# A modulation stream stepped more slowly, and attention's first scores put ahead of the last value transposition

## The chip, the cores and the metric

The kernel runs on one core of a Trainium2 chip. A core has a matrix engine (PE), a vector engine (DVE), a scalar engine (ACT), GpSimd (POOL) and a sync engine (SP) that here issues nearly all DMAs. Each engine takes its instructions strictly in the order in which they were written; engines wait for one another by semaphores. The metric is device time in microseconds (us). Before the change the median of three runs was 2344.88 us (2339.64 to 2345.45).

## The reference, cut to what matters

The program is a transformer block followed by two more mixing layers. Only the first block's first half matters here. With x of 1024 positions by 1024 channels:

```
mod = silu(c) @ w_ada + b_ada                 # 6 x 1024 numbers: shifts, scales, gates
h = modulate(rms_norm(x), mod[0], mod[1])
proj = h @ w_in                               # 25 blocks of 128 columns
o_a = gated linear attention of 4 heads       # q, k, v, r and decay blocks of proj
o_b = softmax attention of 4 heads            # Q, K, V blocks; two score maps a head, a bias on each
x = x + mod[2] * (concat(o_a, o_b) @ w_out)
...                                           # feed-forward with mod[3..5], then the second block
```

The first two parts of `mod` are needed at once. The other four (32 blocks of 128 numbers) are first needed after the softmax attention.

## The kernel before, in words

**phase1** (L428) computes the 25 blocks of `h @ w_in`. Each is 48 fp32r matmuls of 512 columns (L214) into one of two PSUM tiles `ps_g`, and an evacuation (`evac1`, L629) on ACT and DVE: a high part (`ehi`) and a low part (`elo`), which go to DRAM. A `V` block is first copied to an SBUF tile `vt` by ACT, later transposed on PE (`ps_v`, L660) and then split. The last two blocks are K and V of head 3: for these the first half of the columns is done for both, then the second half.

Two background streams are interleaved with these matmuls. Every second contraction step calls `tick`, which lowers each stream's waiting count by its rate; when it is used up, the stream takes one step, and the step says how long to wait for the next one. Stream `bg` runs the heads of the linear attention (`gla_head`): decays by a scan on DVE, exponentials on ACT, small matmuls, a state recurrence of 30 DVE instructions (`sx`), and the output `uh`, `ul`. Stream `bg2`, with rate 0.6, runs the modulation (`ada`, L364): 32 steps, each of which issues the load of the *next* 512 KB weight tile `adw` on SP (two buffers) and then takes one dot product on DVE from the tile that was loaded a step ago (called a dot below). A step returns 2.0, so dots are at least 2.0/0.6 ticks apart.

Between the two halves of the last two blocks, SP issues eight loads for the softmax attention's head 0 (`load_head`) and two biases (`load_bias`). At the end, the last value block's transposition is done (`pend.pop()()`, L607), then `drain` (L608) runs whatever the two streams still have, without matmuls between, and the pools of phase 1 are closed.

**phase2** (L827) is the softmax attention, in 32 steps of 128 queries. `scores` issues 8 matmuls into the two `ps_g` tiles (there called `ps_s`); `expo` adds the bias on DVE (`s`, with the running extreme `mx`) and takes exponentials on ACT; `combine` works on POOL, then PE transposes and the products with the values follow.

Of the kernel before, what the change touches and what calls it, by code (L numbers as in the profile page):

```python
# [10 lines left out]
F32 = mybir.dt.float32  # L11
# [9 lines left out]
T = 1024  # L21
# [99 lines left out]
class Builder:  # L121
# [239 lines left out]
        src = self.bias_d[h, bass.ds(fl * (qb + 1), 1), :, bass.ds((1 - fl) * (128 * qb), T)]  # L361
        self.S.dma_start(out=out, in_=src.rearrange("a p c -> (a p) c"))

    def ada(self, src, n0, n, bias, pairs, pool):  # L364


        ws = deque()

        def load(i):
            if i < n:  # L370
                w = pool.tile([128, D], F32, tag="adw", name="adw", bufs=2)
                self.S.dma_start(out=w, in_=src[n0 + i])
                ws.append(w)

        load(0)
        yield 6.0
        for i in range(n):
            load(i + 1)
            w = ws.popleft()
            for j, (vec, out) in enumerate(pairs):  # L380
                o = w if j == len(pairs) - 1 else pool.tile([128, D], F32, tag="adt", name="adt", bufs=1)
                self.dot(o, w, vec, out[:, i:i + 1])
                yield 2.0 if o is w else 1.0
        for _, out in pairs:
            self.V.tensor_tensor(out=out, in0=out, in1=bias, op=ALU.add)
        yield
# [41 lines left out]
    def phase1(self):  # L428
        nc, tc, V, A, G, S, PE, I = self.nc, self.tc, self.V, self.A, self.G, self.S, self.PE, self.I
# [40 lines left out]
        for half, ps in enumerate(sums):  # L470
            for k in range(8):
                q = nmp.tile([128, 512], F32, tag="nm", name="sq")
# [72 lines left out]
        evp = gl.enter_context(tc.tile_pool(name="evp", bufs=4, reuse_waits="tile"))  # L545
# [14 lines left out]
        self.bg.rate, self.bg2.rate = 0.8, 0.6  # L560
        self.bg2.append(self.lam())
        crow = self.cond_row(self.cond_d, glp, "crow")
        self.bg2.append(self.ada(I["w_ada"], 16, 32, self.vec("b_ada", 16, 32), [(crow, self.mod[:, 16:48])], evp))
        pend = []

        def products(n, ps, **kw):
# [5 lines left out]
        def evac(n, ps):  # L572
            later = self.evac1(order[n], ps, evp)
            if later is not None:
                pend.append(later)

        for n in range(23):
            if n < 3:
                ps = ps0[n]
            else:  # L580
                ps = self.psg.tile([128, T], F32, tag="g", name="ps_g")
# [7 lines left out]
        for half in range(2):  # L589
            for j in range(2):  # L590
                products(23 + j, last[j], halves=(half,))
                if half:
                    self.release(23 + j)
                    evac(23 + j, last[j])
            if not half:
                self.hst[0].close()
                self.heads = {}
                self.hdst = ExitStack()
                self.hpools = [self.hdst.enter_context(tc.tile_pool(name="hdp0", bufs=1, side="right", reuse_waits="tile"))]
                for part in range(8):  # L600
                    self.load_head(0, part)

                self.fl = S.value_load(self.flag[0:1, 0:1], min_val=0, max_val=1)
                self.bias = {}
                for g in range(2):
                    self.load_bias(g, self.ring.tile(("bias", g), [128, T], F32, "bias"))
        pend.pop()()  # L607
        self.drain()  # L608
        gl.close()
        self.hst[1].close()  # L610
        ph.close()
# [17 lines left out]
    def evac1(self, what, ps, evp):  # L629

        nc, V, A, G, S, PE = self.nc, self.V, self.A, self.G, self.S, self.PE
        kind, i = what[0], what[1:]
        if what == "lr":
            self.lr = self.glp.tile([48, T], F32, name="lr")
            A.activation(out=self.lr, in_=ps[0:48], func=ACTF.Copy)
        elif kind in "qk":
            t = evp.tile([128, T], F32, tag="ev", name="ev")
            if kind == "q":
                A.activation(out=t, in_=ps, func=ACTF.Copy, scale=0.125)
            else:  # L640
                V.tensor_copy(out=t, in_=ps)
            S.dma_start(out=self.gqk_d["qk".index(kind), int(i)], in_=t)
        elif kind == "r":
            t = evp.tile([128, T], F32, tag="ev", name="ev")
            A.preload_act_table_set(SET_SILU)
            A.activation(out=t, in_=ps, func=ACTF.Silu)
            A.preload_act_table_set(SET_EXP)
            S.dma_start(out=self.gr_d[int(i)], in_=t)
        elif kind in "vV":


            vt = evp.tile([128, T], F32, tag="ev", name="vt")
            A.activation(out=vt if kind == "v" else vt[:, ::-1], in_=ps, func=ACTF.Copy)

            def later():
                pts = []
                for g in range(2):
                    pt = self.pst.tile([128, 4, 128], F32, tag="t", name="ps_v")
                    for b in range(4):
                        PE.transpose(pt[:, b], vt[:, (4 * g + b) * 128:(4 * g + b + 1) * 128], self.eye)  # L660
                    pts.append(pt)
                if kind == "v":
                    vn = evp.tile([128, 8, 128], F32, tag="ev", name="ev")
                else:
                    hi = evp.tile([128, T], F32R, tag="ev", name="ehi")
                    lo = evp.tile([128, T], F32R, tag="ev", name="elo")
                for g, pt in enumerate(pts):
                    if kind == "v":
                        A.activation(out=vn[:, 4 * g:4 * g + 4], in_=pt, func=ACTF.Copy)
                    else:  # L670
                        h3, l3 = (x[:, g * 512:g * 512 + 512].rearrange("p (b d) -> p b d", b=4) for x in (hi, lo))
                        A.activation(out=h3, in_=pt, func=ACTF.Copy)
                        V.tensor_tensor(out=l3, in0=pt, in1=h3.bitcast(F32), op=ALU.subtract)
                if kind == "v":
                    S.dma_start(out=self.gv_d[int(i)].rearrange("p (b d) -> p b d", b=8), in_=vn)
                else:
                    S.dma_start(out=self.v_d[int(i), 0], in_=hi.bitcast(F32))
                    S.dma_start(out=self.v_d[int(i), 1], in_=lo.bitcast(F32))
            return later
        else:  # L680
            self.split_out(ps, 0.125 if kind == "Q" else 1.0, self.qk_d[int(i), "QK".index(kind)], evp, kind == "K")
        return None
# [26 lines left out]
    def gla_head(self, hd):  # L709
# [114 lines left out]
        S.dma_start(out=self.oa_d[hd, 1], in_=ul.bitcast(F32))  # L824
        yield

    def phase2(self):  # L827

        nc, tc, V, A, G, S, PE = self.nc, self.tc, self.V, self.A, self.G, self.S, self.PE
# [4 lines left out]
        pool = lambda name, bufs, **k: at.enter_context(tc.tile_pool(name=name, bufs=bufs, reuse_waits="tile", **k))  # L834
# [1 line left out]
        bp, self.hvpool, sp, ap, cp = pool("bip", 2), pool("hdv1", 1), pool("sp", 3), pool("atp", 2), pool("acp", 4)  # L836
        trp = at.enter_context(tc.tile_pool(name="trp", bufs=2, space=PSUM))
        NS = 32
        heads, bias, sc, aT, rc = self.heads, self.bias, {}, {}, {}

        def scores(g):
            h, qb = divmod(g, 8)
            q, *kk = heads[h][:3]
            pss = []
            for m in range(2):
                ps = self.psg.tile([128, T], F32, tag="g", name="ps_s")
                for a in range(2):
                    for j in range(2):
                        PE.matmul(ps[:, a * 512:a * 512 + 512], lhsT=q[:, m, qb * 128:qb * 128 + 128],
                                  rhs=kk[j][:, m, a * 512:a * 512 + 512], start=j == 0, stop=j == 1)  # L850
                pss.append(ps)
            sc[g] = pss

        def expo(g):
            mx, sm = (cp.tile([128, 2], F32, tag=t, name=t) for t in ("mx", "sm"))
# [96 lines left out]
        for g in range(-3, NS + 2):  # L952
            if 1 < g + 3 < NS:
                self.load_bias(g + 3, bp.tile([128, T], F32, tag="b", name="bias"))
            if (g + 3) // 8 < 3:
                self.load_head((g + 3) // 8 + 1, (g + 3) % 8)
            if g in (2, 10, 18):
                self.n_max = len(self.seq)
                self.pump(g // 8, -1)
            if g >= 6 and g % 4 > 1 and part < 16:  # L960
                wo_part(part // 8, part % 8)
                part += 1
            if 0 <= g < NS:
                transp(g)
            if 0 <= g + 1 < NS:
                combine(g + 1)
            if 0 <= g - 2 < NS:
                values((g - 2) // 2, g % 2)
            for n in (0,):
                at_step(g, n)  # L970
            if g + 3 < NS:
                scores(g + 3)
            if 0 <= g + 2 < NS:
                expo(g + 2)
                bias.pop(g + 2)
                if g + 2 < 2:
                    self.ring.free(("bias", g + 2))
            if 0 <= g < NS:
                lows(g)
            for n in (4, 3, 2, 1):  # L980
                at_step(g, n)
# [1287 lines left out]
```

## Time and profile before

| | before |
|---|---|
| median of 3 runs | 2344.88 us |
| the profiled execution's own time | 2343.11 us |
| its span | 2341.3 us |
| PE busy | 2188.7 us (93%) |
| DVE busy | 1489.8 us (64%) |
| POOL busy | 1000.9 us (43%) |
| ACT busy | 837.8 us (36%) |
| mean granted PE clock | 0.971 |

The span is what the profile covers; the execution's own time is 1.8 us longer. PE's share is an average over stages. A stage is therefore read by the time in which PE stands still in it, and by what released it. Times in the rows below are counted from the span's start; phase 1's matmuls end near 424 us and the softmax attention starts there.

### The profile page before, as it was taken

Reading aid. Unit: us, or ns where it says so; the run is one execution under the profiler, and the core shown is the slowest. Engines: PE = TensorE matmul, PEld = TensorE weight load, DVE = VectorE, ACT = ScalarE, POOL = GpSimd, SP = SyncE. Lnnn points to the kernel's source line nnn. Section 1 sums busy time; section 2 is a strip of 40 time slices with the busy share of each in tenths; the row PEclk is TensorE's granted clock in tenths of the full one; section 3 lists DMA queues with packets and bytes.
Section 4 is the critical chain, followed back from the end, with each engine's and each line's share of the span. In section 5 each row is a group of like instructions: output and inputs, shape, how many; then the busy total and the mean of one; then the engine's idle time right before and its main releaser. Section 6 shows DMA issues by size and latency. Waiting matters only on the chain. (4 is left out here: it accounts for less than half of the span.)

```text
span 2341.3 us, 28680 instructions
## 1 busy us (share of the span) xinstructions
PE 2188.7 (93%) x10168; PEld 1781.9 (76%) x10168; DVE 1489.8 (64%) x2480; ACT 837.8 (36%) x1371; POOL 1000.9 (43%) x790
## 2 busy tenths in 40 slices
PE   6999998799999999989999998797978999999998
PEld 3777776687877888878787876686866777788886
DVE  8674666589365866799867756849895746221124
ACT  4334332588443222122223335532322444222223
POOL 7333332499443332313465525545543553322243
PEclk8999999899999999999999999898989999999999
DMA  7265664984522344413232424463534624111143
GB/s 269 97 189 201 208 208 158 270 235 149 212 90 99 121 158 153 150 32 101 80 128 90 129 71 134 124 191 134 185 135 138 228 86 149 50 45 51 49 153 117
DMA packets 188838, 326.19 MB, mean 139 GB/s; under 512 B 46818, under 2 KB 87682, under 8 KB 188436
## 3 DMA queue, kind: packets, MB, share of 16 engines
q1 hardware_dynamic: 188400, 324.14, 42.3%
q8 instruction: 80, 1.31, 0.2%
q14 instruction: 66, 0.54, 0.1%
q10 hardware_dynamic: 292, 0.20, 0.0%
HBM read 260.71 MB, written 67.46 MB: 140 GB/s over the span
## 5 line engine op out<-in xcount | busy, mean ns | idle before, releaser
L59 POOL TENSOR_TENSOR lo<-raw,hi 128x512 fp32r<-128x512 f32 (+3 forms) x458 | 561.3, 1238 | 935.4 <-ACT hi L59 511.5
L59 ACT ACTIVATE hi<-raw 128x512 fp32r<-128x512 f32 (+3 forms) x462 | 244.9, 557 | 537.6 <-PE ps_o L214 165.9
L214 PE MATMUL ps_g<-h0hi,hi 128*128 128x512 f32 x568 | 228.5, 402 | 13.3 <-ACT h0hi L59 8.6
L214 PE MATMUL ps_g<-h0lo,hi 128*128 128x512 f32 x568 | 223.5, 393 | 4.7 <-POOL h0lo L59 4.7
L214 PE MATMUL ps_g<-h1lo,hi 128*128 128x512 f32 x568 | 223.4, 393 | 4.7 <-DVE h1lo L59 4.7
L214 PE MATMUL ps_g<-h1hi,hi 128*128 128x512 f32 x568 | 226.8, 399 | 0.0
L214 PE MATMUL ps_g<-h0hi,lo 128*128 128x512 f32 x568 | 223.3, 393 | 1.9 <-DVE lo L59 1.4
L214 PE MATMUL ps_g<-h1hi,lo 128*128 128x512 f32 x568 | 223.2, 393 | 0.0
L59 DVE SCALAR_TENSOR_TENSOR u<-ps_g,vecs,u 128x1023 f32<-128x1023 f32 (+3 forms) x94 | 114.1, 1214 | 93.1 <-ACT u L59 90.4
L214 PEld LDWEIGHTS ps_g<-h0hi,hi 128*128 128x128 f32 x568 | 108.2, 190 | 40.0 <-ACT h0hi L59 9.9
L214 PEld LDWEIGHTS ps_g<-h0lo,hi 128*128 128x128 f32 x568 | 107.8, 190 | 28.7 <-POOL h0lo L59 6.4
L214 PEld LDWEIGHTS ps_g<-h1lo,hi 128*128 128x128 f32 x568 | 107.8, 190 | 28.3 <-DVE h1lo L59 6.0
L214 PEld LDWEIGHTS ps_g<-h0hi,lo 128*128 128x128 f32 x568 | 107.8, 190 | 25.7 <-DVE lo L59 1.8
L214 PEld LDWEIGHTS ps_g<-h1hi,hi 128*128 128x128 f32 x568 | 107.6, 189 | 25.2 <-issue 2.5
L214 PEld LDWEIGHTS ps_g<-h1hi,lo 128*128 128x128 f32 x568 | 107.7, 190 | 22.9
L214 PE MATMUL ps_d<-acthi,hi 128*128 128x512 f32 x272 | 109.2, 401 | 12.0 <-DVE u L59 9.3
L59 DVE TENSOR_TENSOR acc<-acc,sq 128x512 f32<-128x512 f32 x69 | 76.1, 1105 | 52.6 <-ACT sq L59 51.0
L214 PE MATMUL ps_d<-actlo,hi 128*128 128x512 f32 x272 | 107.7, 396 | 0.0
L214 PE MATMUL ps_d<-acthi,lo 128*128 128x512 f32 x272 | 107.6, 396 | 0.0
L59 DVE TENSOR_TENSOR t<-ps_i,rot 64x480 f32<-64x480 f32 (+3 forms) x108 | 64.8, 600 | 38.9 <-PE ps_i L1487 32.7
L59 POOL TENSOR_TENSOR s<-s,s 128x1024 f32<-128x1024 f32 x32 | 77.1, 2410 | 2.7
L59 DVE CUSTOM_DVE_ANT_0 s<-ps_s,bias 128x1024 f32<-128x1024 f32 x64 | 75.7, 1217 | 2.8 <-DMA bias<-bias_d 2.2
(403 smaller groups left out, 5350.5 us busy)
## 6 DMA issues: line engine op xcount, KB each, us to landing
adw<-in_ada_w_dram SPq DMA_DIRECT2D x48, 512.0 KB, 3.5
raw<-in_w_up_dram SPq DMA_DIRECT2D x88, 256.0 KB, 2.8
adw<-in_w_ada_dram SPq DMA_DIRECT2D x32, 512.0 KB, 6.1
bias<-bias_d SPq DMA_DIRECT2D x32, 512.0 KB, 4.3
raw<-in_w_in_dram SPq DMA_DIRECT2D x50, 256.0 KB, 3.9
raw<-in_odd_w_in_dram SPq DMA_DIRECT2D x48, 256.0 KB, 2.6
raw<-in_even_w_in_dram SPq DMA_DIRECT2D x44, 256.0 KB, 4.0
raw<-in_w_down_dram SPq DMA_DIRECT2D x72, 128.0 KB, 2.5
```

Source lines behind the costliest of these rows:

```text
L59: return f(*a, **k)
L214: self.PE.matmul(out, lhsT=a[:, k], rhs=b, start=first and n == 0, stop=last and n == 2)
```

## The change

Three edits. (1) `ada` gets a parameter `lead`, and the first block's modulation stream passes 3.0 where the step's wait was 2.0; the second block's use keeps 2.0. (2) The last value block (`V3`) is copied by ACT into the linear attention's tile `w2` of the pool `glp`, not into one of the four rotating tiles `ev`. (3) `drain` runs first, then the scores of softmax step 0 are issued (the function became a method), and only then the last value block is transposed.

```diff
-    def ada(self, src, n0, n, bias, pairs, pool):
+    def ada(self, src, n0, n, bias, pairs, pool, lead=2.0):
...
-                yield 2.0 if o is w else 1.0
+                yield lead if o is w else 1.0
...
-        self.bg2.append(self.ada(I["w_ada"], 16, 32, self.vec("b_ada", 16, 32), [(crow, self.mod[:, 16:48])], evp))
+        self.bg2.append(self.ada(I["w_ada"], 16, 32, self.vec("b_ada", 16, 32), [(crow, self.mod[:, 16:48])], evp, lead=3.0))
...
+        self.drain()
+
+        self.sc = {}
+        self.scores(0)
         pend.pop()()
-        self.drain()
         gl.close()
...
-            vt = evp.tile([128, T], F32, tag="ev", name="vt")
+
+            end = what == "V3"
+            vt = self.glp.tile([128, T], F32, tag="w2", name="vt") if end else evp.tile([128, T], F32, tag="ev", name="vt")
...
+    def scores(self, g):
+
+        h, qb = divmod(g, 8)
+        q, *kk = self.heads[h][:3]
+        self.sc[g] = []
+        for m in range(2):
+            ps = self.psg.tile([128, T], F32, tag="g", name="ps_s")
+            for a in range(2):
+                for j in range(2):
+                    self.PE.matmul(ps[:, a * 512:a * 512 + 512], lhsT=q[:, m, qb * 128:qb * 128 + 128],
+                                   rhs=kk[j][:, m, a * 512:a * 512 + 512], start=j == 0, stop=j == 1)
+            self.sc[g].append(ps)
...
-            if g + 3 < NS:
-                scores(g + 3)
+            if 0 < g + 3 < NS:
+                self.scores(g + 3)
```

What this moves on the engines is shown at three places.

DVE, where head 3 of the linear attention begins, before: `w` from `ps_z` is the head's decay input, the `adw` rows are dots, the two `smask` rows are the scan, `elo` is the low part of a projected block.

```order
L59 TENSOR_SCALAR w_14932<-ps_z,vecs 128x1024
L59 ISA adw,mod<-adw,crow 128x1024
L59 ISA mod 128x1
L59 ISA adw,mod<-adw,crow 128x1024
L59 ISA mod 128x1
L59 SCALAR_TENSOR_TENSOR w_14974<-smask,w_14932 64x1024 x2
L59 COPY bl<-w_14974 64x16 x2
L59 SCALAR_TENSOR_TENSOR elo<-ps_g,ehi 128x1024
```

The same place on DVE after the change:

```order
L59 TENSOR_SCALAR w_14908<-ps_z,vecs 128x1024
L59 ISA adw,mod<-adw,crow 128x1024
L59 ISA mod 128x1
L59 SCALAR_TENSOR_TENSOR w_14947<-smask,w_14908 64x1024 x2
L59 COPY bl<-w_14947 64x16 x2
L59 ISA adw,mod<-adw,crow 128x1024
L59 ISA mod 128x1
L59 SCALAR_TENSOR_TENSOR elo<-ps_g,ehi 128x1024
```

The second dot has moved from ahead of the scan to behind it, still ahead of `elo`.

DVE at the end of phase 1, before: `mod<-mod` closes the modulation, `ul` ends the linear attention, and the last two rows are the low part of the last value block and the first bias addition of the softmax attention.

```order
L59 TENSOR_TENSOR mod<-mod,vecs 128x32
L59 SCALAR_TENSOR_TENSOR sx<-sx,dec,U 64x128 x6
L59 SCALAR_TENSOR_TENSOR elo<-ps_g,ehi 128x1024
L59 SCALAR_TENSOR_TENSOR w_15414<-ps_o,vecs,ki 128x1024
L59 TENSOR_TENSOR w_15414<-w_15414,sr 128x1024
L59 TENSOR_TENSOR ul<-w_15414,uh 128x1024
L59 TENSOR_TENSOR elo<-ps_v,ehi 128x512 x2
L59 ISA s_15520,mx<-ps_s,bias 128x1024
```

The same place after the change; where lines are left out stand seven more pairs of a dot and its `mod` row.

```order
L59 SCALAR_TENSOR_TENSOR elo<-ps_g,ehi 128x1024
L59 SCALAR_TENSOR_TENSOR w_15388<-ps_o,vecs,ki 128x1024
L59 TENSOR_TENSOR w_15388<-w_15388,sr 128x1024
L59 ISA adw,mod<-adw,crow 128x1024
L59 ISA mod 128x1
L59 TENSOR_TENSOR ul<-w_15388,uh 128x1024
L59 ISA adw,mod<-adw,crow 128x1024
L59 ISA mod 128x1
...
L59 TENSOR_TENSOR mod<-mod,vecs 128x32
L59 TENSOR_TENSOR elo<-ps_v,ehi 128x512 x2
L59 ISA s_15520,mx<-ps_s,bias 128x1024
```

Nine of the 32 dots now stand behind the linear attention's last products, eight of them behind `ul`, and all of them ahead of the first bias addition.

SP's queue at the same end, before, from the second bias on: `qk_d` are the parts of the last K block, `oa_d` the linear attention's output, `v_d` the last value block, `q` and `k` the softmax attention's head 1.

```order
L362 DMA bias<-bias_d 128x1024
L690 DMA qk_d<-ehi 128x1024
L691 DMA qk_d<-elo 128x1024
L823 DMA oa_d<-uh 128x1024
L824 DMA oa_d<-ul 128x1024
L677 DMA v_d<-ehi 128x1024
L678 DMA v_d<-elo 128x1024
L624 DMA q<-qk_d 64x2x1024
```

The same place after the change:

```order
L362 DMA bias<-bias_d 128x1024
L372 DMA adw<-in_w_ada_dram 128x1024
L695 DMA qk_d<-ehi 128x1024
L696 DMA qk_d<-elo 128x1024
L372 DMA adw<-in_w_ada_dram 128x1024
L828 DMA oa_d<-uh 128x1024
L829 DMA oa_d<-ul 128x1024
L372 DMA adw<-in_w_ada_dram 128x1024 x7
L682 DMA v_d<-ehi 128x1024
L683 DMA v_d<-elo 128x1024
L627 DMA q<-qk_d 64x2x1024
```

Nine weight loads stand behind the ten loads for the softmax attention, seven of them behind `oa_d<-ul`. On PE the only move is that the eight transposing matmuls of the last value block stand behind the eight of the first scores.

## Rows read from the trace of the kernel before

**Rows 1.** Busy time of each engine in two stretches of phases 1 and 2.
```profile
core 0: us, PE busy (x) PEld busy (x) DVE busy (x) ACT busy (x) POOL busy (x), PEclk, DMA share, GB/s
190.00:400.00 210.00, 197.38 (x999) 158.84 (x998) 132.09 (x191) 75.14 (x102) 72.53 (x40) 0.98 0.61 211
460.00:600.00 140.00, 136.42 (x850) 115.04 (x849) 117.86 (x235) 115.65 (x219) 123.32 (x100) 0.99 0.69 206
```
**Rows 2.** PE's instructions in order of time, 160 to 375 us: start, length, idle before.
```profile
217.70 0.82 PE L762 MATMUL ps_f<-qi,ki 64*128 64x128 f32 x5 [1.05 <-DVE ki L59]
...
251.67 0.66 PE L805 MATMUL ps_o<-qi,sx 128*128 128x64 f32 x4 [2.18 <-DVE sx L59]
...
365.04 0.50 PE L214 MATMUL ps_g<-h0hi,hi 128*128 128x512 f32 x1 [3.33 <-DVE elo L59]
...
371.35 1.43 PE L762 MATMUL ps_f<-qi,ki 64*128 64x128 f32 x5 [4.64 <-DVE ki L59]
```
**Rows 3.** All engines in order of time, 345 to 369 us (head 3's beginning).
```profile
347.24 2.43 POOL L59 TENSOR_TENSOR w<-w,w 128x1024 f32<-128x1024 f32 x1 [5.22 <-ACT w L59]
...
348.02 1.23 SPq L372 DMA_DIRECT2D adw<-in_w_ada_dram  x2
...
357.58 1.22 DVE L59 CUSTOM_DVE_ANT_0 adw<-adw,crow 128x1024 f32<-128x1024 f32 x1 [10.15 <-DMA adw<-in_w_ada_dram]
...
358.73 4.60 DVE L59 TENSOR_TENSOR_SCAN w<-smask,w 64x1024 f32<-64x1024 f32 x2
...
363.76 1.22 DVE L59 SCALAR_TENSOR_TENSOR elo<-ps_g,ehi 128x1024 fp32r<-128x1024 f32 x1
...
367.93 3.36 DVE L59 TENSOR_TENSOR ki<-k,ki 128x1024 f32<-128x1024 f32 x1
```
**Rows 4.** SP's DMA queue in order of time, 398 to 430 us.
```profile
403.99 0.65 SPq L624 DMA_DIRECT2D q<-qk_d  x1
...
409.92 2.47 SPq L362 DMA_DIRECT2D bias<-bias_d  x2
419.94 0.33 SPq L690 DMA_DIRECT2D qk_d<-ehi  x1
```
**Rows 5.** DMA issues, 400 to 445 us: count, KB each, us from issue to landing.
```profile
qk_d<-ehi SPq DMA_DIRECT2D x1, 512.0 KB, 9.5
```
**Rows 6.** The modulation's weight tile, 150 to 432 us: its DMAs.
```profile
DMA to landing us min/median/max: 3.4/6.1/10.1
```
**Rows 7.** All engines in order of time, 418 to 446 us (phase 1's end).
```profile
422.40 1.22 DVE L59 TENSOR_TENSOR w<-w,sr 128x1024 f32<-128x1024 f32 x1
...
429.53 1.02 ACT L59 ACTIVATE vt<-ps_g 128x1024 f32<-128x1024 f32 x1 [4.82 <-DMA qk_d<-ehi]
...
430.61 1.97 PE L660 MATMUL ps_v<-eye,vt 128*128 128x128 f32 x8 [6.54 <-ACT vt L59]
...
432.67 1.29 DVE L59 TENSOR_TENSOR elo<-ps_v,ehi 128x512 fp32r<-128x512 f32 x2 [6.70 <-PE ps_v L660]
...
434.32 1.23 DVE L59 CUSTOM_DVE_ANT_0 s<-ps_s,bias 128x1024 f32<-128x1024 f32 x1 [0.36 <-PE ps_s L849]
...
444.96 1.23 DVE L59 CUSTOM_DVE_ANT_0 s<-ps_s,bias 128x1024 f32<-128x1024 f32 x1 [2.23 <-DMA bias<-bias_d]
```
**Rows 8.** The second block's modulation, dots and loads in order of time, near 915 us.
```profile
914.18 1.22 DVE L59 CUSTOM_DVE_ANT_0 adw<-adw,cond 128x1024 f32<-128x1024 f32 x1
...
915.44 2.68 SPq L372 DMA_DIRECT2D adw<-in_ada_w_dram  x2
...
919.02 1.23 DVE L59 CUSTOM_DVE_ANT_0 adw<-adw,cond 128x1024 f32<-128x1024 f32 x1 [1.26 <-DMA adw<-in_ada_w_dram]
```
**Rows 9.** Busy time and granted clock in three short stretches, columns as in rows 1.
```profile
428.00:432.00 4.00, 1.39 (x7) 1.39 (x8) 0.00 (x0) 1.26 (x2) 0.00 (x0) 0.54 0.89 363
432.00:436.00 4.00, 4.00 (x13) 3.01 (x12) 2.81 (x5) 1.29 (x3) 0.00 (x0) 0.60 0.50 202
436.00:440.00 4.00, 2.12 (x9) 1.12 (x8) 2.65 (x7) 2.30 (x5) 1.12 (x1) 1.00 1.01 246
```

More of the change, by code (lines that the diff above doesn't have):

```diff
@@ L838, in phase2 @@
         NS = 32
[L839 to L852, printed above, removed]
+        heads, bias, sc, aT, rc = self.heads, self.bias, self.sc, {}, {}
         def expo(g):
```

## The prediction, made before the changed kernel was timed

> **What bounds the kernel now.** I read the busy time by stretches first, then PE's own order of time for the places where it stood still, then what DVE, SP's queue and the DMAs did at those places. PE is busy 197.38 of 210 us in the middle of phase 1 and 136.42 of 140 us in the softmax attention [rows 1]: in both stages it is PE that sets the pace. So an edit gains only what it takes out of PE's idle time, and a start of the softmax attention that is late by some amount is not made good later, since PE has 3.6 us of slack in 140.
>
> In phase 1 the idle of PE that DVE causes lies at a few places [rows 2]: 1.05 us for `ki`, 2.18 us for the recurrence `sx`, then 3.33 us for an `elo` and 4.64 us for `ki` of head 3. The two last have one cause. A dot had its load issued at 348.02 and started only at 357.58, after 10.15 us in which DVE did nothing; scan, `elo`, `qi` and `ki` stand behind it [rows 3]. At the end, PE waits 6.54 us for the copy `vt`, and that for a rotating tile, until the write `qk_d<-ehi` has landed (4.82 us) [rows 7].
>
> **Change part by part.** *The slower stream, in phase 1.* The number of dots is the same, 32; nine of them move out of phase 1's matmuls to its end. What that frees, place by place:
>
> - Head 3's beginning. The scan needs POOL's `w`, done at 347.24 + 2.43 = 349.67. Without a second dot ahead of it, scan and its small copies take 349.7 to 354.7 (in the old place 358.73 to 363.76, 5.03 us) [rows 3]. The next dot still waits for the same load until 357.58 and ends at 358.73. `elo` then ends at 359.9 where it ended at 365.0, and PE, which was there at 365.04 - 3.33 = 361.7, doesn't wait. `qi` and `ki`, which at this size take about 1.2 us as `elo` does, follow; `ki` ends at 362.3, or at 364.5 if it takes 3.36 us as before. PE would be there at 371.35 - 4.64 - 3.33 = 363.4. So 8.0 us are gained, or 6.9 us with the long `ki`. I take 8.0.
> - 217.70: one dot fewer stands between scan and `qi`, at 1.22 us or more each; the wait of 1.05 us goes. 251.67: one dot fewer stands ahead of the second half of `sx`: 1.2 us of the 2.18 us go.
>
> Sum: 8.0 + 1.05 + 1.2 = 10.2 us earlier at the end of phase 1. As bounds I keep 6 us (the long `ki`, and one of the small ones staying) and 12 us. Nothing else that PE waits for moves, since PE's own order is the same up to the last matmul. In what follows I count on the clock of the old trace and take the 10.2 us off at the end.
>
> *The drained dots.* They are the cost, and they stand ahead of the first bias addition on DVE, which works in order. Call the nine dots 23 to 31. Load 23 is issued right behind the second bias, at 409.92 + 2.47 = 412.4. Ahead of it in the queue are ten loads of 512 KB issued from 403.99 on [rows 4]. When they were through is seen from the next DMA in line: `qk_d<-ehi`, issued at 419.94, landed 9.5 us later, at 429.4 [rows 5]. Load 23 now takes that place, so I put dot 23 at 430.0, though DVE could take it at 422.40 + 1.22 = 423.6 [rows 7].
>
> From there each of the two buffers goes round: dot, load, dot. The nearest place in the trace where exactly that is the limit is the second block's modulation: a dot at 914.18, its buffer's load at 915.44, the next dot on it at 919.02, having waited 1.26 us for the load: 4.84 us a round, 3.58 us from issue to landing [rows 8]. Dots 23, 25, 27, 29, 31 are on one buffer, four rounds; the first of them also waits for `ul` (1.22 us, as the product before it) and its write's issue (0.33 us), because load 25 stands behind these on SP. So dot 31 starts at 430.0 + 1.55 + 4 x 4.84 = 450.9 and ends at 452.1; the other buffer is done before. With the closing addition (0.2 us) and the value block's low part (1.29 us), the first `s` starts at 453.6 where it started at 434.32 [rows 7]: 19.3 us later.
>
> Bounds: if a load takes the 3.4 us that is the least in phase 1, the four rounds are 0.7 us shorter; if the median of 6.1 us, 4 x 2.5 = 10 us longer [rows 6]. If load 23 is not held up and dot 23 comes at 423.6, everything is 6.4 us earlier. So the cost lies between 12 and 29 us; I take 19.3, since at the end the queue holds little beside these loads, as near 915 us.
>
> *The copy into `w2` and the scores ahead.* `vt` no longer waits 4.82 us; PE does scores and transposition some 5 us earlier. But both end at DVE, and the value block's low part and the first `s` now stand behind dot 31. The gain of 6.5 us that these two edits could have is hidden wholly behind the drain. What is left is 0.36 us in which `s` waited for PE, and part of the 2.23 us that a bias load made a later `s` wait [rows 7]: `v_d<-ehi` is then written while the dots run, ahead of head 1's loads and not among them. I take 1.5 us gained, between 0 and 2.6.
>
> *The matrix clock.* [...] I take 1 us lost, between 0 and 4.
>
> [...]
>
> **Sum.** -10.2 + 19.3 - 1.5 + 1.0 = +8.6 us on the profiled execution's 2343.11, so 2351.7 us. Its own time lies 1.8 us under the median of the three runs, within their spread of 5.8 us; on the median it is 2353.5. I say 2353 us.
>
> **Rivals.**
>
> *The loads overtake.* If load 23 shares the DMA engines with the ten loads ahead and does not queue behind them, DVE never stands still for it and the tail costs 19.3 - 6.4 - 0.7 = 12.2 us. With the gains whole (10.2 and 2.6) and no clock lost the sum is -0.6 us: 2344 us, not slower. It decides from dot 23's start: the change breaks even when that is at 424.4 or less on the old clock and nothing else is lost. For it: ten loads of 512 KB between 404 and 429 are some 210 GB/s, while 363 are seen from 428 to 432 [rows 9], so the DMA engines had room. Against it: `qk_d<-ehi` took 9.5 us in just this place. Chance 0.22; to be faster by more than 0.3% it would need some 6 us beyond this.
>
> *The drain runs at phase 1's pace.* If the loads take 6.1 us at the end too, because writes of the K block and the linear attention's output go with them, the sum is +8.6 + 10 = 2364 us. For it: four writes of 512 KB are issued among the first loads. Against it: they are four, and the last five loads have the queue to themselves. Chance 0.12.
>
> *The cold start costs more.* [...] Chance 0.10.
>
> *The gain in phase 1 doesn't come.* PE is freed at head 3 but meets another late operand soon after, and only 3 us stay: 2360 us. Chance 0.06.
>
> **How the numbers follow.** My own case has 0.50, with 2348 to 2359. The others reach from 2344 to 2364. The range of 2342 to 2363 leaves out about 2 in 10. About 0.3%, 7 us, is what a measurement of this kernel can tell from no change: faster is below 2338, slower above 2352. My own case at 2353.5 lies just above that line, so 0.3 of its 0.50 count as slower and 0.2 as the same; with the three dearer rivals whole, 0.58 are slower. Of the overtaking rival 0.12 are the same; 0.10 I give to faster, for gains that I don't see. So the same has 0.32 and faster 0.10.
>
> **What would show it.** Right: the dot at head 3 no longer stands ahead of the scan and PE's waits of 3.33 and 4.64 us are gone; phase 1's last matmul ends near 414 instead of 424; nine dots follow one another at 2.4 to 2.7 us a dot behind `ul`, each pair waiting for its loads; the first `s` starts near 443.5; PE stands still from about 418 until then; from there on the steps are as before, some 9 us late. Wrong: dots of the drain back to back at 1.3 us, a first `s` at or before 434, or a softmax attention that makes the delay good.

## The result, and the profile after

The changed kernel takes 2356.62 us (median of five runs, 2354.05 to 2362.46), the kernel before 2344.88 us (five runs, 2339.58 to 2345.45): a ratio of 1.0051, with an interval of 1.0034 to 1.0068. The profiled execution of after took 2362.46 us, 19.35 us more than that of before; its span is 2360.7 us, its mean granted clock 0.966 where it was 0.971. It is the slowest of its five runs, so differences between the two profiles are larger than the one between the medians. A later comparison, with 12 and 35 runs, gave 2356.76 us for the same changed kernel, and for before a median of 2353.11 us with runs from 2341.29 to 2369.20: a ratio of 1.0014, 0.9995 to 1.0033, which can't be told from 1. The changed kernel comes out alike both times; it is the kernel before that varies, and a part of this document is about that.

**Phase 1.** What PE waited for between 150 and 460 us in the profile after: us in total, times, longest.

```profile
PE ps_s L841 <- DVE mx L59: 28.7, 2, 28.4
PE ps_o L810 <- DVE sx L59: 5.0, 4, 1.9
PE ps_f L767 <- DVE ki L59: 1.5, 1, 1.5
```

The wait of 3.33 us for `elo` is gone, that of 4.64 us for `ki` is down to 1.51, that of 1.05 us at 217.70 is gone, and the one of 2.18 us for `sx` is still 1.94 us [rows 2]. At the end one long wait has come: behind the last value block's transposition PE stands still for 28.4 us.

DVE at head 3's beginning in the profile after, the place of [rows 3]:

```profile
350.27 1.22 DVE L59 CUSTOM_DVE_ANT_0 adw<-adw,crow 128x1024 f32<-128x1024 f32 x1
...
353.77 4.60 DVE L59 TENSOR_TENSOR_SCAN w<-smask,w 64x1024 f32<-64x1024 f32 x2 [2.28 <-POOL w L59]
...
361.57 2.32 DVE L59 CUSTOM_DVE_ANT_0 adw<-adw,crow 128x1024 f32<-128x1024 f32 x1 [0.81 <-DMA adw<-in_w_ada_dram]
...
363.82 1.21 DVE L59 SCALAR_TENSOR_TENSOR elo<-ps_g,ehi 128x1024 fp32r<-128x1024 f32 x1
364.96 2.51 DVE L59 TENSOR_TENSOR qi<-q,qi 128x1024 f32<-128x1024 f32 x1
367.39 1.21 DVE L59 TENSOR_TENSOR ki<-k,ki 128x1024 f32<-128x1024 f32 x1
```

No dot stands ahead of the scan any more, and the wait for a weight is 0.81 us instead of 10.15. The scan starts 5 us earlier (353.77, it was 358.73). But `ki` starts only 0.54 us earlier (367.39, it was 367.93). The larger part of that is no matter of head 3: this execution comes to it some 4.1 us late. The same matmuls of head 2, before and then after:

```profile
304.84 1.16 PE L787 MATMUL ps_u<-vn,ki 64*128 64x128 f32 x8 [0.21 <-ACT ki L59]
```

```profile
308.94 1.16 PE L792 MATMUL ps_u<-vn,ki 64*128 64x128 f32 x8 [0.21 <-ACT ki L59]
```

With these 4.1 us taken off, the scan starts at 349.7 and the dot at 357.5, both as forecast, and `ki` ends at 364.5, where the forecast had 362.3 or, with a long `ki`, 364.5: the dot took 2.32 us and `qi` 2.51 us, where it had counted 1.2 each. So of PE's two waits here, 7.97 us, 6.5 us are gained.

**The end of phase 1.** SP's queue in the profile after, the place of [rows 4]; the second number is the time over which the issues went.

```profile
398.62 0.65 SPq L627 DMA_DIRECT2D q<-qk_d  x1
...
409.13 0.34 SPq L372 DMA_DIRECT2D adw<-in_w_ada_dram  x1
...
417.38 0.34 SPq L372 DMA_DIRECT2D adw<-in_w_ada_dram  x1
...
426.05 16.63 SPq L372 DMA_DIRECT2D adw<-in_w_ada_dram  x7
442.78 0.38 SPq L682 DMA_DIRECT2D v_d<-ehi  x1
...
451.57 0.36 SPq L362 DMA_DIRECT2D bias<-bias_d  x1
```

DVE there, the place of [rows 7]:

```profile
423.28 1.22 DVE L59 CUSTOM_DVE_ANT_0 adw<-adw,crow 128x1024 f32<-128x1024 f32 x1 [5.09 <-DMA adw<-in_w_ada_dram]
...
431.51 1.23 DVE L59 CUSTOM_DVE_ANT_0 adw<-adw,crow 128x1024 f32<-128x1024 f32 x1 [3.29 <-DMA adw<-in_w_ada_dram]
...
446.81 1.23 DVE L59 CUSTOM_DVE_ANT_0 adw<-adw,crow 128x1024 f32<-128x1024 f32 x1 [2.03 <-DMA adw<-in_w_ada_dram]
...
449.38 1.22 DVE L59 CUSTOM_DVE_ANT_0 s<-ps_s,bias 128x1024 f32<-128x1024 f32 x1
...
461.24 1.23 DVE L59 CUSTOM_DVE_ANT_0 s<-ps_s,bias 128x1024 f32<-128x1024 f32 x1 [3.67 <-DMA bias<-bias_d]
```

Head 0's first load stands 403.99 - 398.62 = 5.4 us earlier than before, the first bias addition 449.38 - 434.32 = 15.1 us later. So from the load to the addition it takes 50.76 us where it took 30.33: 20.4 us more. The seventh addition starts at 465.41, 16.4 us late, the last of the softmax attention 19.9 us late; from there to the end both spans are alike (after 1758.6 us, before 1759.0). The 3.5 us that come on after the seventh addition go with six further waits for biases, 5.1 us in all, where before had none. The second profile of the changed kernel, made with the experiments, had none there either and the last addition 15.6 us late: these six belong to that one execution.

### The profile page after: what moved, and what is told of

Same layout as the page of the kernel before. It is cut to its first block, busy times and chain, and to the rows that moved or that the text cites. A ratio compares the mean times of both kernels' runs of the same rounds, so it can differ in the third digit from the quotient of the medians.

```text
span 2360.7 us, 28676 instructions
## 1 busy us (share of the span) xinstructions
PE 2190.7 (93%) x10168; PEld 1782.0 (75%) x10168; DVE 1491.0 (63%) x2480; ACT 836.9 (35%) x1371; POOL 997.6 (42%) x790
## 5 line engine op out<-in xcount | busy, mean ns | idle before, releaser
L841 PE MATMUL ps_s<-k,q 128*128 128x512 f32 x256 | 71.0, 418 | 35.7 <-DVE mx L59 35.0
L841 PEld LDWEIGHTS ps_s<-k,q 128*128 128x128 f32 x256 | 47.2, 198 | 50.4 <-issue 28.6
```

What stands on the lines that cost most here:

```text
L841: self.PE.matmul(ps[:, a * 512:a * 512 + 512], lhsT=q[:, m, qb * 128:qb * 128 + 128], rhs=kk[j][:, m, a * 512:a * 512 + 512], start=j == 0 ...
```

## The experiments

The runs came in four groups (the first four of the table, the next four, then three, then one), each with its own runs of the kernel before on the same chip; ratios are to these.

| run | median us (lowest to highest) | before there | ratio (interval) |
|---|---|---|---|
| edits 2 and 3, lead 2.0 | 2350.36 (2343.44 to 2356.67) | 2349.54 | 1.0008 (0.9991 to 1.0026) |
| lead 3.0 alone | 2354.86 (2348.22 to 2358.89) | 2349.54 | 1.0022 (1.0006 to 1.0038) |
| changed, lead 2.25 | 2345.13 (2334.61 to 2353.30) | 2349.54 | 0.9979 (0.9959 to 0.9999) |
| changed, nine dots left out | 2334.90 (2328.96 to 2340.56) | 2349.54 | 0.9947 (0.9930 to 0.9964) |
| changed, again | 2356.76 (2351.34 to 2362.03) | 2353.11 | 1.0014 (0.9995 to 1.0033) |
| changed, last eight dots without loads | 2344.52 (2342.58 to 2349.00) | 2353.11 | 0.9963 (0.9944 to 0.9982) |
| edits 2 and 3, V3's parts moved too | 2347.02 (2339.17 to 2361.46) | 2353.11 | 0.9984 (0.9959 to 1.0009) |
| before with a matmul added | 2345.89 (2340.63 to 2348.92) | 2353.11 | 0.9963 (0.9942 to 0.9984) |
| lead 2.25, parts moved, matmul | 2343.37 (2340.82 to 2349.50) | 2349.98 | 0.9979 (0.9961 to 0.9997) |
| the same, later loads | 2343.86 (2338.29 to 2355.30) | 2349.98 | 0.9966 (0.9947 to 0.9986) |
| the same, second matmul | 2341.70 (2336.89 to 2348.20) | 2349.98 | 0.9963 (0.9947 to 0.9979) |
| lead 2.15, bias ahead of head 1 | 2343.34 (2338.02 to 2346.06) | 2351.03 | 0.9960 (0.9937 to 0.9982) |

### Which edit does it

The changed kernel with the old lead (the diff), the kernel before with the new lead alone, and the changed kernel with 2.25 in the same place:

```diff
-        self.bg2.append(self.ada(I["w_ada"], 16, 32, self.vec("b_ada", 16, 32), [(crow, self.mod[:, 16:48])], evp, lead=3.0))
+        self.bg2.append(self.ada(I["w_ada"], 16, 32, self.vec("b_ada", 16, 32), [(crow, self.mod[:, 16:48])], evp, lead=2.0))
```

> The last value block copied into w2 and the first scores ahead of its transposition, but the modulation stepped with 2.0 as before. Theory (the drained dots are the cost): no dot is left for the drain, phase 1 keeps its waits (3.33 and 4.64 us at head 3) and ends near 424 us; the copy no longer waits 4.8 us, so the first bias addition starts when its bias has landed, at 427 to 429 instead of 434.3; total about 6 us under the kernel before, 2337 to 2341 us. Rival (the scores ahead or the copy cost something themselves, or the attention's start is set by other DMAs): the first bias addition at 434 or later, total 2345 us or more.

> The modulation stepped with 3.0, the two other edits undone. Theory: the drain hides what the two edits gain, so this is as slow as the changed kernel: first bias addition at 448 to 451 us, total 2353 to 2360 us, the same within 0.2%. Rival (the edits' gain of 6 us comes on top even with the drain): 2361 to 2365 us. Second rival (most of the loss is made by the two edits, not by the step): 2345 us or less.

> All three edits, with 2.25 in place of 3.0: by the order of instructions one dot is left behind the last K block's low part, and at head 3 one dot stands ahead of the scan instead of two. Theory: the wait of 4.64 us for ki and the one of 3.33 us for elo at head 3 shrink to under 2 us together, the copy does not wait, and there is nearly no drain: total 2328 to 2335 us, faster than both kernels. Rival (phase 1 does not give these back, because PE meets its clock's drops or another late operand): as without the slower step, 2337 to 2341 us.

Edits 2 and 3 alone give 1.0008, the lead alone 1.0022. The two intervals overlap, so it is the profiles that tell them apart: from head 0's first load to the seventh bias addition it takes 65.5 us with the lead alone (397.66 to 463.14), 46.2 us with edits 2 and 3 alone (411.62 to 457.84) and 45.0 us before. The lead is what makes the late start. The lead alone came out as expected (first addition at 450.72 us); of edits 2 and 3 alone 2337 to 2341 us were expected, and the rival's 2345 us or more came. They don't gain because the low part of the last value block, right ahead of the first bias addition, waits for something else. DVE with edits 2 and 3 and the old lead:

```profile
437.80 1.29 DVE L59 TENSOR_TENSOR elo<-ps_v,ehi 128x512 fp32r<-128x512 f32 x2 [4.15 <-DMA qk_d<-elo]
439.00 1.22 DVE L59 CUSTOM_DVE_ANT_0 s<-ps_s,bias 128x1024 f32<-128x1024 f32 x1
...
452.17 1.23 DVE L59 CUSTOM_DVE_ANT_0 s<-ps_s,bias 128x1024 f32<-128x1024 f32 x1 [4.98 <-DMA bias<-bias_d]
```

The copy `vt` has left the rotating tiles, the value block's two parts have not: `elo` waits 4.15 us for the write `qk_d<-elo` to leave its tile, as `vt` waited 4.82 us for `qk_d<-ehi`. From head 0's first load (411.62) to the first addition it takes 27.4 us instead of 30.3. Those 2.9 us then go into the wait for the third bias, 4.98 us where it was 2.23 [rows 7].

With a lead of 2.25 only one dot is left behind head 0's loads, and the time is some 0.2% under before. That is neither the 2328 to 2335 us of the theory nor the rival's 2337 to 2341: at head 3 PE still waited 3.66 us for `ki`.

### What the drain costs

First, the changed kernel with 23 of the 32 dots:

```diff
-        self.bg2.append(self.ada(I["w_ada"], 16, 32, self.vec("b_ada", 16, 32), [(crow, self.mod[:, 16:48])], evp, lead=3.0))
+        self.bg2.append(self.ada(I["w_ada"], 16, 23, self.vec("b_ada", 16, 32), [(crow, self.mod[:, 16:48])], evp, lead=3.0))
```

> The changed kernel with only the first 23 of the 32 dots and their loads; the last nine columns of the modulation are left at zero. Theory: the drain is the whole loss, about 20 us behind phase 1's last matmul: first bias addition at 421 to 425 us instead of 449.4, total 2356.6 minus 24 to 28, so 2329 to 2333 us. Rival (the late start is set by the loads of head 0 and the biases, or the clock after the idle costs most): first bias addition at 435 or later, total 2342 us or more.

Second, the changed kernel once more beside one whose last eight dots are done on a tile that is there already:

```diff
-                self.S.dma_start(out=w, in_=src[n0 + i])
+                if lead < 3.0 or i < 24:
+                    self.S.dma_start(out=w, in_=src[n0 + i])
...
-                self.dot(o, w, vec, out[:, i:i + 1])
+                self.dot(o, w if lead < 3.0 or i < 24 else vec, vec, out[:, i:i + 1])
```

> The changed kernel itself, for a comparison with the others on one chip. Theory: 20 us above the version that leaves nine dots out and as slow as the slower step alone, so 0.2 to 0.5% above the kernel before; in its trace the first bias addition again starts some 50 us after the first load of head 0 is issued (398.6 to 449.4 us in the first profile). Rival (the first comparison of 0.5% was mostly chance of the clock): within 0.1% of the kernel before.

> The changed kernel with the last eight dots taken from the condition row itself, so that they need no load (their eight columns of the modulation are not the reference's). Theory (the round trip of a load through two buffers sets the drain, not the dots): the eight dots follow back to back at 1.25 us, 10 us instead of the 22.2 us from 426.99 to 449.2; only dot 23 still waits for its load behind the loads of head 0. First bias addition 11 to 13 us earlier than in the changed kernel, total 9 to 13 us under it. Rival (DVE's work is what the drain costs): under 4 us gained.

DVE in the run without the last eight loads; the dots between follow at 1.15 us each:

```profile
427.48 1.23 DVE L59 CUSTOM_DVE_ANT_0 adw<-adw,crow 128x1024 f32<-128x1024 f32 x1 [5.34 <-DMA adw<-in_w_ada_dram]
...
429.77 1.22 DVE L59 CUSTOM_DVE_ANT_0 adw<-crow 128x1024 f32<-128x1024 f32 x1
...
437.79 1.22 DVE L59 CUSTOM_DVE_ANT_0 adw<-crow 128x1024 f32<-128x1024 f32 x1
...
440.36 1.22 DVE L59 CUSTOM_DVE_ANT_0 s<-ps_s,bias 128x1024 f32<-128x1024 f32 x1
```

The first and the seventh addition without the nine dots:

```profile
426.22 1.21 DVE L59 CUSTOM_DVE_ANT_0 s<-ps_s,bias 128x1024 f32<-128x1024 f32 x1
...
444.27 1.23 DVE L59 CUSTOM_DVE_ANT_0 s<-ps_s,bias 128x1024 f32<-128x1024 f32 x1 [1.04 <-PE ps_s L843]
```

From head 0's first load to the seventh addition it takes 66.8 and 67.4 us in the two profiles of the changed kernel (398.62 to 465.41 and 397.99 to 465.36), 53.4 us without the eight loads (402.57 to 455.97) and 45.7 us without the nine dots (398.56 to 444.27). So the nine dots cost 21.1 us there by the first profile and 67.4 - 45.7 = 21.7 us by the second; of the latter 67.4 - 53.4 = 14.0 us are the eight loads' round trips and the other 53.4 - 45.7 = 7.7 us the dots themselves and the first one's wait for its load. The medians say the same: 2356.76 - 2344.52 = 12.2 us for the loads and, across two groups, 2356.76 - 2334.90 = 21.9 us for the nine dots. Without the nine dots the first addition (426.22) and the median lie 1 to 2 us above what was expected. Without the eight loads the 12.2 us lie within the 9 to 13 expected, while the first addition came 9.4 us earlier (440.36 against 449.77), not 11 to 13. The changed kernel's own 1.0014 lies between its theory (0.2 to 0.5% above before) and its rival (within 0.1%).

### Where edits 2 and 3 lose their gain

Edits 2 and 3 with the old lead, and the two parts of V3 also in tiles of the linear attention:

```diff
-                    hi = evp.tile([128, T], F32R, tag="ev", name="ehi")
+                    src = [self.glp.tile([128, T], F32, tag=t, name=n).bitcast(F32R) for t, n in (("qi", "ehi"), ("w0", "elo"))] if end else None
+                    hi = src[0] if end else evp.tile([128, T], F32R, tag="ev", name="ehi")
...
```

> The step at 2.0, the copy in w2 and the scores ahead, and now the two parts of the last value block outside the rotating tiles as well. Theory: in the run without the slower step the low part waited 4.15 us until the last K block's write had landed and only freed its tile then; that wait goes and the first bias addition comes 3 to 4 us earlier, some 24 us after the first load of head 0 instead of 27.4. But the third bias still lands some 36 to 38 us after that load, so the later steps gain nothing: total within 0.15% of the kernel before. Rival (the low part's tile was what took the edits' gain): 0.2 to 0.3% faster than before.

The wait of 4.15 us is gone, and the first addition comes 25.2 us after head 0's first load (30.3 before). The seventh still comes 44.7 us after it (45.0 before), because the third bias lands when it landed before. The ratio of 0.9984 can't be told from 1, nor from the rival's 0.2 to 0.3%. A last run therefore put that bias ahead of head 1's loads; it has the moved parts, the matmul of the next section and a lead of 2.15 beside:

```diff
-            if (g + 3) // 8 < 3:
-                self.load_head((g + 3) // 8 + 1, (g + 3) % 8)
+            if 0 <= g + 1 < 24:
+                self.load_head((g + 1) // 8 + 1, (g + 1) % 8)
```

> As the run with a lead of 2.25, the parts of V3 moved and the added matmul, with two edits more: a lead of 2.15, by which the last weight load is issued ahead of head 0's loads, and head 1's loads two steps later, so that the third bias's load is issued ahead of all of them. Theory: what the last value block's edits gain is given back because the third bias lands behind head 1's first three loads (it landed 11.8 us after its issue in the run with 2.25, 8.4 us in the kernel before). Then it lands some 5 to 6 us after its issue, the third step waits under 2 us instead of 6.95, and from head 0's first load to the seventh bias addition it takes 38 to 41 us instead of 44 to 46; the time is some 0.2% under that of the run with 2.25, a ratio near 0.995 to 0.996. Rival: the bias's load is slow by itself and by the writes of the value block that stand ahead of it in either order; then the seventh bias addition is 44 to 46 us behind the first load as ever, the time as with 2.25, a ratio near 0.998. Third: head 1's operands come too late, and PE waits for them at the ninth step; then the ratio is 1.0 or more and PE shows a wait of several us for q or k.

The third step's addition in this run, which started with no wait:

```profile
445.75 1.22 DVE L59 CUSTOM_DVE_ANT_0 s<-ps_s,bias 128x1024 f32<-128x1024 f32 x1
```

This bias landed 5.1 us after its issue; it took 13.0 us with the parts moved, 11.7 us in the run with 2.25 and the parts moved, and 8.3 us before. It was issued about as long after head 0's first load as before (32.0 and 32.6 us), and the value block's writes stand ahead of it in both, so these writes are not what holds it up. The seventh addition came 13.2 us after the first (437.62 to 450.85), with the parts moved and the bias behind head 1's loads 19.4 us, before 14.7 us; a part of that is only that the first one came later. The bias that lands sooner is the mechanism of the first theory. Its number for the seventh addition, 38 to 41 us after head 0's first load, was missed: it came after 44.4 us, since the first one came 31.1 us after it, against 25.2. Most of these 5.9 us went to the clock, by an estimate that takes PE's pace to go with it (0.43 us a matmul at 0.50 and 0.23 us at 1.00, next section): it was at 0.74, 0.50 and 0.50 in the three stretches of 4 us from 412, so 1.0 + 2 + 2 = 5 us. The ratio of 0.9960 agrees with the theory's and doesn't exclude the rival's 0.998. PE waited 0.6 us for head 1's `k`, so the third case didn't happen.

### The clock in phase 1

Each stop of PE at an output of the linear attention was met with a matmul that needs nothing late, in the kernel before:

```diff
         o = self.pss.tile([128, T], F32, tag="s", name="ps_o")
+        PE.matmul(o[:, 0:512], lhsT=self.ones, rhs=qi[:, 0:512], start=True, stop=True)
```

> The kernel before with one more matmul of 512 columns in fp32 (overwritten at once) ahead of each linear head's output, where PE stands still 1.0 to 2.2 us for the state recurrence. Theory (such a stop of some 2 us lets the granted clock fall to half for 10 to 13 us in some executions, as near 252 us in four of six profiles, and this is a good part of the spread between executions): no slot under 0.97 within 20 us behind the four outputs' starts, the total 2 to 6 us lower. Rival (the clock falls for another reason, and the filler only adds work): the same or up to 2 us slower, with the same clock drops.

Why this was tried: the second head's output by stretches of 4 us, in the profile of before and then of after. The last four rows are the start of the softmax attention after. Columns are the stretch, its length, busy time (and instructions) of PE, PEld, DVE, ACT and POOL, the granted clock, DMA share and GB/s.

```profile
248.00:252.00 4.00, 1.82 (x11) 1.43 (x10) 3.45 (x11) 0.00 (x0) 0.00 (x0) 1.00 0.76 252
252.00:256.00 4.00, 4.00 (x38) 4.00 (x37) 2.34 (x4) 0.00 (x0) 0.00 (x0) 1.00 0.44 151
```

```profile
248.00:252.00 4.00, 2.43 (x11) 2.44 (x12) 2.62 (x6) 0.00 (x0) 0.00 (x0) 0.71 0.21 80
252.00:256.00 4.00, 4.00 (x20) 4.00 (x20) 0.00 (x0) 0.00 (x0) 0.00 (x0) 0.50 0.00 0
256.00:260.00 4.00, 4.00 (x20) 3.90 (x20) 0.00 (x0) 0.36 (x1) 0.00 (x0) 0.50 0.00 0
260.00:264.00 4.00, 4.00 (x11) 2.48 (x9) 0.00 (x0) 0.93 (x2) 0.00 (x0) 0.59 0.00 0
...
428.00:448.00 20.00, 0.00 (x0) 0.00 (x0) 8.80 (x16) 0.00 (x0) 0.00 (x0) 0.50 0.67 215
448.00:452.00 4.00, 1.25 (x3) 1.09 (x4) 3.71 (x9) 1.30 (x3) 0.00 (x0) 0.50 0.53 147
452.00:456.00 4.00, 3.78 (x11) 2.21 (x11) 2.67 (x6) 2.37 (x5) 2.19 (x2) 0.69 0.95 218
456.00:460.00 4.00, 2.16 (x12) 1.40 (x12) 0.41 (x2) 2.18 (x4) 3.92 (x4) 1.00 1.04 256
```

Before stopped 2.18 us for `sx` and kept a granted clock of 1.00; after stopped 1.94 us and then worked at 0.50 until about 263, with PE busy all the time. At 0.50 the `ps_g` matmuls of 512 columns followed one another at 0.43 us (259.94 to 261.64), at 1.00 at 0.23 us (264.63 to 267.81). The `ps_u` matmuls shown above start 4.1 us later after, though after was 2.1 us ahead at 250 (249.57 against 251.67): the fall cost 4.1 + 2.1 = 6.2 us. That is more than the stop.

With the matmul the ratio to before is 0.9963, and the 12 runs lie within 8.3 us where 35 runs of before lie within 27.9. Its profile has a stop of 1.32 us ending at 253.61 and no fall behind it. It has falls near 141, 220, 302 and 370 us, none of them at an output; the profile of before has only those near 141 and 370, and none at an output either, so these two profiles alone show no effect.

All profiles together show one. Nine have no added matmul: there the stop at the second head's output lasts 1.93 to 2.19 us, and in six of them (after, its second profile, edits 2 and 3, lead 2.25, nine dots left out, eight loads left out) the clock falls to 0.50 within 2 us of its end, for 10 to 14 us; in three (before, the lead alone, V3's parts moved) it doesn't. Five have the matmul, four of them with other edits beside: the stop lasts 1.15 to 1.33 us, and none falls there. The granted clock of each run points the same way: over the 35 runs of before it goes from 0.963 to 0.976 and the time falls as it rises (correlation -0.82); its mean is 0.967, and 0.970 in the 12 runs with the matmul. That these falls are the whole gain of 0.37% is not shown.

Three versions built on this, one after the other: a lead of 2.25 with the moved parts and the matmul; then the linear attention's `vn` loaded only behind the product `ks`, and `sr` only ahead of `sq`; then a second such matmul in the linear attention's scores (the last two lines of the diff).

```diff
-        S.dma_start(out=vn, in_=self.gv_d[hd].rearrange("p (b d) -> p b d", b=8))
-        S.dma_start(out=sr, in_=self.gr_d[hd])
...
+        S.dma_start(out=vn, in_=self.gv_d[hd].rearrange("p (b d) -> p b d", b=8))
...
+        S.dma_start(out=sr, in_=self.gr_d[hd])
...
+            if g == 0:
+                PE.matmul(pf.rearrange("p j c -> p (j c)"), lhsT=self.ones, rhs=q2[:, 0:512], start=True, stop=True)
```

> The step at 2.25, the last value block's copy and parts outside the rotating tiles, the scores ahead, and the filler matmul ahead of each linear head's output. Theory: the filler takes the clock's drops behind the four outputs away (worth 0.4% on the kernel before), the step of 2.25 shortens the stops at head 3 (3.3 and 4.6 us), with one dot left for the end: 0.4 to 0.7% under the kernel before, all executions within 12 us of each other. Rival (the slower step gains nothing once the clock doesn't fall): as the filler alone, 0.3 to 0.4%.

> As the last one, and each linear head's values and output gates (512 KB each) are loaded when they are needed, not in its first step ahead of the modulation's weight tile. Theory: the weight tile at head 3, which landed 9.5 us after its issue behind 2 MB of the head's loads, lands 3 to 4 us earlier, and the stop of PE for ki there shrinks from 3.7 to under 1.5 us: 0.1 to 0.2% under the last kernel. Rival (the values are then late for the state products): a new wait of PE or DVE for vn, the same or slower.

> As the last one, with a second filler matmul ahead of the first product of each linear head, where PE stops 1.0 to 4.6 us for ki and where the clock fell near 140, 220 and 370 us in most profiles. Theory: fewer drops there, 1 to 4 us gained, since each costs 4 to 6 us and the filler hides in the stop. Rival (four fillers of 0.9 us that are not hidden at head 2 and elsewhere): the same or 2 us slower.

None of the three is clearly under the matmul alone, and the first, with a ratio of 0.9979, missed both its theory and its rival. It gives away its earlier start: the first addition at 430.77, then 6.95 us for the third bias. The second missed what was expected of head 3; DVE there, and at the end:

```profile
352.01 1.23 DVE L59 CUSTOM_DVE_ANT_0 adw<-adw,crow 128x1024 f32<-128x1024 f32 x1 [5.53 <-DMA adw<-in_w_ada_dram]
...
353.17 6.60 DVE L59 TENSOR_TENSOR_SCAN w<-smask,w 64x1024 f32<-64x1024 f32 x2
...
364.37 3.36 DVE L59 TENSOR_TENSOR ki<-k,ki 128x1024 f32<-128x1024 f32 x1
...
426.59 1.23 DVE L59 TENSOR_TENSOR w<-w,sr 128x1024 f32<-128x1024 f32 x1 [7.36 <-DMA sr<-gr_d]
```

The dot came 5.6 us earlier than in [rows 3], but the scan took 6.60 us instead of 4.60 and `ki` 3.36 again, and PE still waited 4.5 us for `ki`. The later load of `sr` stands behind head 0's ten loads and makes a new wait of 7.36 us. In the third the wait for `ki` is 3.4 us and the clock still fell there, to 0.61 and 0.54 in the two stretches of 4 us from 368. Of the ten profiles ahead of these three versions all had such a fall between 140 and 153 us, three had one near 220 and five one between 364 and 385.

## Why the prediction was right

It said 2353 us, 2342 to 2363, most likely slower; the time is 2356.62 us. The mechanism is the one forecast: dots left for the end stand ahead of the first bias addition, and their loads' round trips set the pace there. The sizes are another matter. At the seventh addition the profiles differ by -5.4 + 20.4 + 1.4 = 16.4 us, where 8.6 us were forecast; the medians differ by 11.7 us in the first comparison and by 3.7 us in the later one. The forecast lies between these, and that 2353 us came so near to the median is in part luck.

- **Phase 1, -10.2 us forecast.** Head 0's first load came 5.4 us earlier in the two profiles. Over all profiles with a lead of 3.0 it came at 399.1 us in the mean (five: 398.62, 397.99, 397.66, 398.56, 402.57), over before and the two runs with 2.0 and no added matmul at 407.3 (403.99, 411.62, 406.42): 8.3 us. The stall behind the weight at head 3 went as said. What was mis-sized is the time to `ki`, for which the forecast took operations of 1.2 us from [rows 3]: the dot and `qi` took 2.3 and 2.5 us, so 1.51 us of the wait stayed. Of the 1.2 us expected at the recurrence `sx`, 0.24 us came (2.18 to 1.94). And the fall of the clock at 250 took 6.2 us; no step had it. In turn before lost time to a fall that after doesn't have: late in its stop of 4.64 us for `ki` the clock fell, and three stretches of 4 us from 368 have 0.79, 0.50 and 0.86, where after has 1.00. So the 5.4 us are gains and falls together.
- **The drained dots, +19.3 us forecast.** 20.4 us by the two profiles, 21.1 to 21.7 us by the experiments. Dot 23 waited 5.09 us for its load, as concluded from [rows 5]; on the old clock it came at 423.28 + 5.4 = 428.7, forecast 430.0. The pace taken from [rows 8] was too fast: by 4.84 us a round dot 31 would have come at 423.28 + 1.55 + 4 x 4.84 = 444.2, and it came at 446.81, so (446.81 - 423.28 - 1.55) / 4 = 5.5 us a round. The two differences, -1.3 and +2.6 us, make up about the 1.1 us by which this profile's 20.4 us lie above 19.3. The bounds of 12 and 29 us hold it.
- **The start, -1.5 us forecast.** There is nothing. The drain hid edits 2 and 3, as forecast, but they have no gain without the drain either: first `elo` for the K block's write, then the third bias takes it back. In after that bias is waited for 3.67 us, 1.4 us more than in [rows 7]: a sign wrong, and small.
- **The clock at the restart, +1 us forecast.** That 1 us was the author's estimate, and no run shows it. What the profile of after shows is a wait of 28.4 us, the clock at 0.50 from 428 to 452, at 0.69 in the next 4 us and at 1.00 in the stretch from 456. From the first to the seventh addition it takes 16.0 us, before, which had 0.54 and 0.60 for 8 us there [rows 9], 14.7; the difference is the bias's 1.4 us. So up to there the longer idle of PE cost nothing that can be seen.

The fall of 250 to 263 came behind a stop of 1.94 us. The prediction could have weighed such falls for phase 1's short stops, as the trace of before shows one in the stop of 4.64 us (0.79, 0.50 and 0.86 from 368). But 1.94 us of idle with a fall in after, and 1.94 and 2.18 us without one in the lead alone and in before, show that the length of the stop alone doesn't decide here.

The rivals: the loads didn't overtake (the break-even point of that rival is, by its own terms, 423.6 + 0.6 = 424.2 us, not 424.4), since dot 23 waited 5.09 us in one profile and 4.99 in the other. The drain did not run at phase 1's pace: its rounds took 5.5 us, between the 4.84 forecast and the 4.84 + 2.5 = 7.3 us of that rival. The cold start cost no more: about 0 us, as said above. That the gain in phase 1 would not come was half true: 5.4 us in the one profile, 8.3 us in the mean.

What stays open is how far before itself is disturbed. In the four later groups its median is 2349.5 to 2353.1 us, in the first comparison 2344.9; the change costs between 0.1 and 0.5% by that. Whether that is chance or the chip used is not shown. And 21.1 us for the dots less the mean gain of 8.3 us in phase 1 leave 12.8 us, more than either difference of the medians: where the rest goes is open.

## What to carry to other kernels

A background stream that is slowed down ends later, and what doesn't fit before the stage ends is paid there at the round trip of its buffers (here 5.5 us for two dots of 1.2 us), with the busiest engine waiting: count the steps that are left behind, and lower the rate only as far as none are. An edit that frees a late operand gained nothing here while the next late one behind it, a rotating tile and then a bias load, was not freed too. Where a busy PE makes short stops, look at the granted clock behind them before weighing the stops themselves (here a stop of 1.94 us was followed by a fall that cost 6.2 us).

## What the runs showed of the hardware

The clock's fall behind a short stop is not the same from one execution to the next. At the second head's output a stop of 1.93 to 1.94 us was followed by a fall to 0.50 in both profiles of the changed kernel, one of 1.94 us with the lead alone and one of 2.18 us in before were not. Two neighbouring stretches of the last run, columns as above, show one more such fall:

```profile
408.00:412.00 4.00, 2.26 (x10) 1.39 (x8) 3.74 (x11) 0.00 (x0) 0.00 (x0) 1.00 0.93 203
412.00:416.00 4.00, 3.70 (x24) 3.70 (x25) 1.48 (x3) 0.00 (x0) 1.47 (x1) 0.74 1.05 210
```

PE stopped 2.04 us for `sx` at 410 to 412, with the clock at 1.00, and it was at 0.50 from 416 to 424, while PE was busy all the time. This run has the added matmul, so the matmul doesn't rule such a fall out where the stop stays near 2 us. The two falls weighed here cost 6.2 us and, by the estimate above, some 5 us, more than most edits here give.
